# The last token tiles of a transformer trunk: tile 2's LayerNorm on VectorE with plain stores, in place of ScalarE with an adding transfer

## The chip, the cores and the metric

One core of one Trainium2 chip runs the whole program. The metric is the device time of one execution in microseconds. The kernel before takes 1698.73 us (median of three runs, 1698.60 to 1699.02).

A core has five engines that run their own instruction queues and wait for each other by semaphores: TensorE (PE in the profile; PEld is its weight load), VectorE (DVE), ScalarE (ACT), GpSimd (POOL) and SyncE (SP). SyncE here does nothing but issue transfers. Transfers issued by SyncE run in the hardware queue (q1), those issued by GpSimd in the software queue (q0). Only the ones from GpSimd can add to what already lies at the destination. Both queues share the same 16 transfer engines.

## The reference, cut to what matters

The reference is a trunk of two layers on 512 tokens of width 1024. Each layer ends with a channel sublayer and a LayerNorm over it:

```python
def layer_norm(x, g, b):
    mu = jnp.mean(xf, axis=-1, keepdims=True)
    var = jnp.mean(jnp.square(xf - mu), axis=-1, keepdims=True)
    y = (xf - mu) * lax.rsqrt(var + LN_EPS) * g + b

for i in range(DEPTH):
    ...                                       # token sublayer: attention, retention, merge, LayerNorm 1
    ffn = conv_glu_ffn(x, w_up[i], conv_w[i], conv_b[i], w_down[i])
    ple = jax.nn.sigmoid(x @ w_ple_gate[i]) * (p[i] @ w_ple_proj[i])
    x = layer_norm(DEEPNORM_ALPHA * x + ffn + ple, ln2_g[i], ln2_b[i])
return x
```

The change concerns the very last line of the last layer: `layer_norm(...)` with `ln2_g` and `ln2_b`, whose result is the program's output.

## The kernel before, in words

All matrix products are float32. Each operand is split into two parts, `hi` (a cast on ScalarE) and `lo` (a subtraction on VectorE), and each product is three matmuls. Weights come in pieces of 512 KB: SyncE loads them in the order of one long list (`Stream`), and GpSimd adds a second piece to some of them with adding transfers (`Stream.add`), since the down projection and two other products use a block scheme with seven products (`a`, `c`, `t1`, `t2`, `d`, `t3`, `t4`) in place of eight.

Tokens are rows. The 512 tokens are four tiles of 128 partitions. For the last sublayer of a layer, `R[0]` to `R[3]` hold the four row tiles (128 x 1024) of the sum that goes into LayerNorm 2. The down projection runs in three segments (`SEGS`), and in the last one (`fin`) of the last layer (`last`) each `R[t]` becomes final and is normalised. Within these parts every engine's instructions stand in the order in which the code issues them (`_Ordered`), so the order of the calls is the order of the work on each engine.

The halves of the tiles become final in this order: tiles 0 and 1 after product `d`, tiles 2 and 3 after `t4`, which yields tile 2 first and tile 3 half a product later. The functions that the end is made of:

- `stats(t, cb)`: VectorE's sums of one half of tile t. `moments(t)`: mean and variance from the two halves, then `rstd_of`: variance + eps on VectorE (`ve`), its power -1/2 on GpSimd (`rstd`).
- `norm_gb(t)`, for tiles 0 and 1: ScalarE computes (R - mean) * rstd in one pass, GpSimd multiplies by the gain `g2c`.
- `send(t)`: GpSimd issues an adding transfer of `R[t]` (512 KB) to `out`. For this, rows of `out` are filled with the bias beforehand: at line 1129, at the start of the last layer's channel sublayer, SyncE writes the bias row to all rows of tiles 0, 1 and 2.
- `norm_g(t)`: VectorE, whole tile: (R - mean) * gain. `norm_b(t)`: VectorE, in two halves: R * rstd + bias, each half followed by a plain transfer (256 KB) that SyncE issues.

In the kernel before, tiles 0 and 1 take `norm_gb` and `send`. Tile 2 takes `norm_g` on VectorE, a scaling by rstd on ScalarE, and `send(2)`. Tile 3 takes `norm_g` and `norm_b`. On GpSimd the end of the queue is: rstd of tile 2, `send(1)`, `send(2)`, rstd of tile 3.

SyncE's transfers rotate through eight completion semaphores, and each one waits, where needed, for the transfer that used its semaphore last. At the end of the program (line 1584) every engine drains, SyncE waits for all transfers to have landed, and two barriers follow.

Of the kernel before, what the change touches and what calls it, by code (L numbers as in the profile page):

```python
# [10 lines left out]
AF = mybir.ActivationFunctionType  # L11
# [91 lines left out]
def trunk(tc, wpack, x_nat, x_tr, head, p_tr, rpb, decay, ln_par, ln_col, conv, cos_t, sin_t, dist, xi_d, zd, mask, ident_d, out):  # L103
    nc = _Engines(tc)
# [3 lines left out]
    with ExitStack() as es:  # L108
# [14 lines left out]
        def nm(s):  # L123
            cnt[0] += 1
            return f"{s}_{cnt[0]}"
# [4 lines left out]
        def unit_f(s, shape=(P, 1024)):  # L130
            return up.tile(list(shape), F32, tag="u", name=nm(s))
# [273 lines left out]
        def drain(g):  # L405
            for _ in g:
                pass
# [171 lines left out]
        def ple_half(l, cb):  # L579

            if cb == 0:
                pk[:] = [unit_f("pp") for _ in range(4)]

            def keep(t, ps):
                nc.scalar.copy(pk[t][:, cb * 512:(cb + 1) * 512], ps)

            lh = lambda k, s, t: ptr[l][k][:, s, t * P:(t + 1) * P]
            if l or cb:
                drain(gemm_n(lh, 1, [], post=keep))
                return  # L590

            hi, lo = ws.get()
            pss = [bank("gn") for _ in range(4)]
            for k in range(2):
                r = slice(k * 512, (k + 1) * 512)
                for t in range(4):
                    for s in range(2):
                        nc.tensor.matmul(pss[t], lh(k, s, t), hi[:, r], start=k == s == 0, stop=False)
                for t in range(4):
                    nc.tensor.matmul(pss[t], lh(k, 0, t), lo[:, r], start=False, stop=k == 1)  # L600
                    if k:
                        keep(t, pss[t])
# [11 lines left out]
        for l in range(DEPTH):  # L614
# [511 lines left out]

            if last:

                for t in range(3):
                    nc.sync.dma_start(out[t * P:(t + 1) * P, :], ln_par[l, 3:4, :].to_broadcast([P, D]))  # L1130

            R = [unit_f("R") for _ in range(4)]
# [155 lines left out]
            for s, n in enumerate(SEGS):  # L1288
# [39 lines left out]
                def into(t, c, ps, op=ALU.add):  # L1328
                    nc.vector.tensor_tensor(R[t][:, c], R[t][:, c], ps, op)

                def stats(t, cb):
                    if fin:
                        nc.vector.bn_stats(st[t][:, cb, :], R[t][:, (N1, N2)[cb]])
# [8 lines left out]
                mv, rs, nmr = {}, {}, {}  # L1342

                def moments(t):
                    mv[t] = small("mv", 2)
                    nc.vector.bn_aggr(mv[t], st[t])
                    rs[t] = rstd_of(mv[t][:, 1:2], LN_EPS, 1)

                def norm(t, R=R):
                    nc.vector.tensor_scalar(R[t], R[t], mv[t][:, 0:1], rs[t], op0=ALU.subtract, op1=ALU.mult)  # L1350
# [10 lines left out]
                def send(t, R=R):  # L1361

                    nc.gpsimd.dma_start(out[t * P:(t + 1) * P, :], R[t], accum_op=ALU.add)

                def norm_g(t, R=R):
                    nc.vector.scalar_tensor_tensor(R[t], R[t], mv[t][:, 0:1], g2c, op0=ALU.subtract, op1=ALU.mult)

                def norm_b(t, R=R):
                    for c in (N1, N2):
                        nc.vector.scalar_tensor_tensor(R[t][:, c], R[t][:, c], rs[t], b2c[:, c], op0=ALU.mult, op1=ALU.add)  # L1370
                        nc.sync.dma_start(out[t * P:(t + 1) * P, c], R[t][:, c])

                def out_pair(t, xt, xf, R=R):
                    h = t // 2
                    for k in range(4):
                        if k % 2 == 0:
                            xf[h, k // 2] = unit_f("xf", (P, 2, 2, 256))
                        ps = bank("tr")
                        f = xf[h, k // 2][:, k % 2]
                        for q in range(2):  # L1380
                            for i in range(2):
                                nc.tensor.transpose(ps[:, (2 * q + i) * P:(2 * q + i + 1) * P], R[t + i][:, (k + 4 * q) * P:(k + 4 * q + 1) * P], ident)
                        for q in range(2):
                            kk = k + 4 * q
                            nc.scalar.activation(f[:, q, :], ps[:, q * 256:(q + 1) * 256], AF.Identity, bias=gb[:, 1, kk:kk + 1], scale=gb[:, 0, kk:kk + 1])
                    yield
                    for k in range(4):
                        ts = slice(t * P, (t + 2) * P)
                        split(xt[:, k:k + 5:4, 0, ts], xt[:, k:k + 5:4, 1, ts], xf[h, k // 2][:, k % 2])
                    yield  # L1390
# [46 lines left out]
                for k in BOUND if not last else ("t4a", "t4b"):  # L1437
                    if k[0] == "p":
                        ple_half(l + 1, int(k[1]))
                    elif k == "tr":  # L1440
                        ws.xw = None
                        xt = xp.tile([P, 8, 2, 512], F32R, tag="xt", name=nm("xt"))
                        xf = {}
                        drain(out_pair(0, xt, xf))
                    else:
                        i = "ab".index(k[2]) + 2
                        next(t4)
                        into(i, N1, x4[i - 2])
                        stats(i, 0)
                        moments(i)  # L1450
                        if not last:
                            norm(i)
                            nc.sync.dma_start(scr[i * P:(i + 1) * P, :], R[i])
                        elif i == 2:
                            send(1)
                            norm_g(2)
                            nc.scalar.activation(R[2], R[2], AF.Copy, scale=rs[2])
                            send(2)
                if last:
                    norm_g(3)  # L1460
                    norm_b(3)
            pending = out_pair
# [125 lines left out]
```

## Time and profile before

| | us |
|---|---|
| runs, median (lowest to highest of 3) | 1698.73 (1698.60 to 1699.02) |
| the profiled execution's own time | 1698.33 |
| its span, first to last instruction | 1696.5 |
| TensorE busy | 1679.7 |
| end of the last matmul, from the span's start | 1681.7 |
| end of VectorE's last instruction | 1687.7 |
| `send(0)`, `send(1)`, `send(2)`: issued by GpSimd at | 1678.42, 1682.06, 1684.73 |
| and landed after | 5.3, 6.6, 6.7 |
| plain halves of tile 3: issued by SyncE at | 1687.03, 1687.69 |
| and landed after | 4.9, 4.9 |
| pre-fill of tiles 0, 1, 2 with the bias: issued from 1271.91, landed after | 12.2, 14.6, 14.8 |

Times within the profile are counted from the span's start. The profiled execution is one run; its time is 1.8 us above its span, and 0.4 us below the median of the three runs. In rows of the timeline the columns are start, duration, engine, line, operation, output <- inputs, shape, count, and in brackets the idle time before it and what ended it. Most operations carry line 86, the helper that fixes the order, so they are told apart by their tiles: `R` is a row tile, `lng` and `lnb` gain and bias, `mv` the moments. A `q` behind an engine's name (POOLq, SPq) is its instruction queue: issuing, waiting and draining, not computing.

### The profile page before, as it was taken

How to read it: one execution, taken by the hardware profiler on the slowest of the kernel's cores; microseconds unless marked ns; L12 is line 12 of the kernel's file. 1: busy time of each engine (PE TensorE's matmuls, PEld its weight loads, DVE VectorE, ACT ScalarE, POOL GpSimd, SP SyncE). 2: the span in 40 equal slices, each digit the busy share in tenths (PEclk: the TensorE clock that was granted, in tenths of full speed). 3: DMA queues.
4: the chain of work that ended last, by engine and by line, in shares of the span. 5: the costliest groups of instructions: out<-in, count | busy, mean ns of one | idle time of the engine just before them, and what ended most of it. 6: DMA issues, size and time to landing. Idle time of an engine off the chain costs nothing.

```text
span 1696.5 us, 20952 instructions
## 1 busy us (share of the span) xinstructions
PE 1679.7 (99%) x7895; PEld 1404.1 (83%) x7895; DVE 1251.7 (74%) x1870; ACT 903.5 (53%) x1345; POOL 125.7 (7%) x143
## 2 busy tenths in 40 slices
PE   9999999999999999999999999999999999999996
PEld 7888888888888888888888888888888888888885
DVE  6768778657787767667875787776678887676777
ACT  6755557654366444345575654666444573443442
POOL 1100000000200100000112000000002010010012
PEclk9999999999999999999999999999999999999998
DMA  8953222344656535526779322232466464274274
GB/s 299 257 161 106 87 81 90 103 143 152 196 137 160 123 113 161 140 98 181 205 210 231 117 78 91 72 109 93 161 212 194 123 174 115 84 200 123 82 214 90
DMA packets 73397, 244.52 MB, mean 144 GB/s; under 512 B 8528, under 2 KB 11088, under 8 KB 73296
## 3 DMA queue, kind: packets, MB, share of 16 engines
q1 hardware_dynamic: 58464, 191.27, 32.9%
q0 software_dynamic: 14832, 51.91, 17.4%
q8 instruction: 62, 1.02, 0.2%
q14 instruction: 39, 0.32, 0.1%
HBM read 228.47 MB, written 14.16 MB: 143 GB/s over the span
## 4 chain that ended last, share of the span: by engine, by line
PE 92%; DVE 3%; issue 2%; DMA 1%; ACT 1%; POOL 1%; SPq 0%; POOLq 0%; DVEq 0%; ACTq 0%
PE gt L86 29%; PE u L86 12%; PE gt L363 8%; PE gt L364 8%; PE gt L365 8%; PE v L86 6%; PE w L86 3%; PE gn L365 3%; PE gn L363 3%; PE gn L364 3%; PE x L86 1%; PE gn L86 1%; PE na L983 1%; PE pt L971 1%; DVE lo L86 1%
## 5 line engine op out<-in xcount | busy, mean ns | idle before, releaser
L86 PE MATMUL gt<-x1t,hi 128*128 128x512 f32 x1408 | 433.4, 389 | 0.0
L86 PEld LDWEIGHTS gt<-x1t,hi 128*128 128x128 f32 x1408 | 264.3, 188 | 54.9
L86 PE MATMUL gt<-x1t,lo 128*128 128x512 f32 x704 | 274.1, 389 | 0.1
L86 DVE TENSOR_TENSOR lo<-raw,hi 128x1024 fp32r<-128x1024 f32 (+1 forms) x155 | 185.5, 1207 | 44.7 <-ACT hi L86 44.2
L86 DVE SCALAR_TENSOR_TENSOR ca<-gt,cw,ca 128x511 f32<-128x511 f32 x176 | 131.8, 749 | 79.0 <-ACT ca L86 75.9
L156 ACT CAST hi<-raw 128x1024 fp32r<-128x1024 f32 x96 | 100.9, 1051 | 146.9 <-issue 80.5
L86 ACT CAST hi<-raw 128x1024 fp32r<-128x1024 f32 (+1 forms) x155 | 159.7, 1040 | 34.3 <-PE u L86 14.4
L363 PE MATMUL gt<-xt,hi 128*128 128x512 f32 x416 | 163.5, 393 | 0.0
L157 DVE TENSOR_TENSOR lo<-raw,hi 128x1024 fp32r<-128x1024 f32 x96 | 117.4, 1223 | 62.3 <-ACT hi L156 61.7
L364 PE MATMUL gt<-xt,hi 128*128 128x512 f32 x416 | 162.2, 390 | 0.0
L365 PE MATMUL gt<-xt,lo 128*128 128x512 f32 x416 | 162.1, 390 | 0.0
L86 PEld LDWEIGHTS gt<-x1t,lo 128*128 128x128 f32 x704 | 132.1, 188 | 28.3 <-DVE lo L86 1.0
L86 ACT ACTIVATE ca<-gt,cw 128x512 f32<-128x512 f32 x88 | 68.6, 780 | 131.0 <-PE gt L86 131.0
L86 DVE TENSOR_TENSOR lo<-rawa,hi 128x1024 fp32r<-128x1024 f32 x90 | 104.7, 1175 | 42.8 <-ACT hi L86 42.3
L86 ACT CAST hi<-rawa 128x1024 fp32r<-128x1024 f32 x90 | 90.0, 1015 | 37.9 <-DMA rawa<-in_wpack 18.8
L365 PEld LDWEIGHTS gt<-xt,lo 128*128 128x128 f32 x416 | 78.1, 188 | 16.6
L363 PEld LDWEIGHTS gt<-xt,hi 128*128 128x128 f32 x416 | 78.2, 188 | 15.0
L364 PEld LDWEIGHTS gt<-xt,hi 128*128 128x128 f32 x416 | 78.2, 188 | 14.8
L86 POOL DMA_DIRECT2D rawa<-in_wpack x68 | 61.3, 916 | 340.0 <-DVE lo L86 295.2
L86 PE MATMUL gt<-xt,hi 128*128 128x512 f32 x192 | 59.2, 389 | 0.0
L86 PE MATMUL v<-hi,sa 128*128 128x512 f32 x176 | 56.1, 389 | 0.0
L413 POOL TENSOR_TENSOR rstd<-ve,mhalf 128x2 f32<-128x2 f32 (+1 forms) x24 | 23.3, 972 | 369.0 <-DVE ve L411 369.0
(322 smaller groups left out, 3556.2 us busy)
## 6 DMA issues: line engine op xcount, KB each, us to landing
raw<-in_wpack SPq DMA_DIRECT2D x247, 512.0 KB, 3.8
rawa<-in_wpack POOLq DMA_DIRECT2D x66, 512.0 KB, 6.4
rawa<-in_wpack SPq DMA_DIRECT2D x22, 512.0 KB, 6.4
rawt<-in_wpack SPq DMA_DIRECT2D x22, 512.0 KB, 6.5
rawt<-in_wpack POOLq DMA_DIRECT2D x22, 512.0 KB, 7.7
r_scr<-pp SPq DMA_DIRECT2D x8, 512.0 KB, 9.8
g_scr<-sga SPq DMA_DIRECT2D x16, 256.0 KB, 4.4
sab<-g_scr SPq DMA_DIRECT2D x16, 256.0 KB, 4.0
```

Source lines behind the costliest of these rows:

```text
L86: r = f(*a, **k)
L156: nc.scalar.copy(hi, src)
L157: nc.vector.tensor_sub(lo, src, _f(hi))
L363: nc.tensor.matmul(ps, lh, rh, start=start, stop=False, skip_group_check=more)
L364: nc.tensor.matmul(ps, lh, rl, start=False, stop=False, skip_group_check=more)
L365: nc.tensor.matmul(ps, ll, rh, start=False, stop=stop, skip_group_check=more)
L413: nc.gpsimd.tensor_tensor(r, v, mhalf[:, :n], ALU.pow)
L971: nc.tensor.transpose(ps[:, i * P:(i + 1) * P], S[:, g * 256 + bb * P:g * 256 + (bb + 1) * P], ident)
L983: nc.tensor.matmul(ov[kt], lv, pt[kt // 2][:, sp_, c], start=i == 0 and sp_ == 0, stop=i == 3 and sp_ == 1)
```

## The change

Tile 2 is treated as tile 3 is. Its rows of `out` are not filled with the bias beforehand, ScalarE's scaling and `send(2)` are gone, and `norm_b(2)` is called where tile 3's moments have been computed and `norm_g(3)` is about to be. Tiles 0 and 1 stay as they are.

```diff
             if last:
-                for t in range(3):
+                for t in range(2):
                     nc.sync.dma_start(out[t * P:(t + 1) * P, :], ln_par[l, 3:4, :].to_broadcast([P, D]))
...
                         elif i == 2:
                             send(1)
                             norm_g(2)
-                            nc.scalar.activation(R[2], R[2], AF.Copy, scale=rs[2])
-                            send(2)
                 if last:
+                    norm_b(2)
                     norm_g(3)
                     norm_b(3)
```

On the engines this gives: SyncE one transfer less at the start of the sublayer and two more at the end, ahead of tile 3's two; ScalarE one instruction less; GpSimd one transfer less, so that rstd of tile 3 follows `send(1)`; VectorE two half-tile instructions more, between tile 3's `ve` and `norm_g(3)`. The order of everything else is the same.

## The prediction

> **What bounds the kernel now.** I read the page first, then the last 18 us of the chain of waits, the order of work there, the landings of the transfers to `out`, and the instructions that close the program (line 1584).
>
> The page: TensorE is busy 99% of the span.
>
> ```profile
> span 1696.5 us, 20952 instructions
> ...
> PE 1679.7 (99%) x7895; PEld 1404.1 (83%) x7895; DVE 1251.7 (74%) x1870; ACT 903.5 (53%) x1345; POOL 125.7 (7%) x143
> ```
>
> So only two things can move the time: a hole in TensorE's row, or the tail behind its last matmul, which ends at 1681.7. The tail is 14.8 us. The chain of waits there (start, duration, what) runs through GpSimd: its rstd of tile 2, ScalarE's scaling of tile 2, the issue of the third adding transfer, and only then VectorE's last step.
>
> ```profile
> 1681.41 1.85 POOL rstd L86
> 1683.26 0.02 issue
> 1683.28 1.16 ACT R L86
> 1684.44 0.29 issue
> 1684.73 0.86 POOL out L86
> 1685.59 0.64 POOLq L1584
> 1686.23 0.03 issue
> 1686.25 0.75 DVE R L86
> ```
>
> The timeline shows the same end by engine: the reader is to see VectorE idle for 0.45 us at 1685.8, because rstd of tile 3 stands in GpSimd's queue behind the transfer at 1684.73.
>
> ```profile
> 1684.53 1.28 DVE L86 SCALAR_TENSOR_TENSOR R<-R,mv,lng 128x1024 f32<-128x1024 f32 x1
> 1684.73 0.86 POOL L86 DMA_DIRECT2D out<-R  x1 [0.61 <-ACT R L86]
> 1685.30 0.92 POOL L86 TENSOR_TENSOR rstd<-ve,mhalf 128x1 f32<-128x1 f32 x1
> 1686.25 1.41 DVE L86 SCALAR_TENSOR_TENSOR R<-R,rstd,lnb 128x512 f32<-128x512 f32 x2 [0.45 <-POOL rstd L86]
> 1687.03 1.11 SPq L86 DMA_DIRECT2D out<-R  x2
> ```
>
> But compute is over at 1687.7 and the span lasts to 1696.5. The closing instructions of line 1584 (count, then ns min/median/max, then first and last start):
>
> ```profile
> L1584 POOLq DRAIN  x3: 40/93/10982, 1684.7 to 1696.2; - x3
> L1584 SPq DRAIN  x3: 7/7/7, 1692.8 to 1696.0; - x3
> ```
>
> SyncE, which waits for every transfer, is done at 1692.9. GpSimd's first drain starts at 1684.7 and takes 10.98, so it ends at 1695.7; 0.77 of barriers follow. What SyncE waited for (total, times, longest) agrees: 3.3 us for transfers, then 3.0 at the barrier.
>
> ```profile
> SPq L1584 <- DMA out<-R: 4.1, 3, 3.3
> SPq L1584 <- PEq L1584: 3.5, 2, 3.0
> ```
>
> So **GpSimd's drain ends the program**, 2.8 us behind everything else. It ends 4.25 us after the third adding transfer has landed (issued 1684.73, landing 6.74 later: 1691.47) and 9.5 us after GpSimd's last instruction (rstd of tile 3, 1686.22). VectorE's drain, in contrast, ends 0.05 us after its last instruction.
>
> The plain transfers: the two halves of tile 3 landed 4.9 us after issue.
>
> ```profile
> L86 SPq DMA_DIRECT2D out<-R x2: 344/397/450, 1687.0 to 1687.7; - x2
> ...
> DMA to landing us min/median/max: 4.9/4.9/5.0
> ```
>
> The same 256 KB from SBUF to HBM, with nothing beside it, landed in 2.0.
>
> ```profile
> L781 SPq DMA_DIRECT2D g_scr<-sga x1: 326/326/326, 1032.5 to 1032.5; - x1
> ...
> DMA to landing us min/median/max: 2.0/2.0/2.0
> ```
>
> From 1688.4 to 1690.5 the adding queue (q0) had the engines, and only 6 plain packets ran (queue, packets, MB, share of the engines).
>
> ```profile
> q0 software_dynamic: 109, 0.42, 101.0%
> q1 hardware_dynamic: 6, 0.01, 1.8%
> ```
>
> **The change part by part.** Its order of instructions is otherwise unchanged on all five engines.
>
> *The pre-fill of tile 2's rows (one of three at 1271.9).* SyncE issues 0.8 us less and 512 KB less moves. What hides it: TensorE was busy 40.00 of 40 us from 1260 to 1300 and 99.93 of 100 in the next 100, so no gain. Every later SyncE transfer shifts by one in the rotation of eight completion semaphores, but each still waits for the transfer eight before it. If the cover went, the holes of that stretch are the measure: 0.07 us. I take 0, with ±0.3 from the spread of the runs (1698.60 to 1699.02).
>
> *ScalarE's scaling (1.15) and the third adding transfer (0.86 of GpSimd, 512 KB).* Both leave the chain. On the transfer engines the adding queue's work from 1688.4 to 1690.9 disappears.
>
> *rstd of tile 3.* GpSimd's queue is free at 1684.1, when the second adding transfer is issued (1682.06 + 2.05); the input is ready at 1684.61. The four rows of this operation in the tail take 0.55, 0.56, 0.92 and 1.83, so it ends between 1685.2 and 1686.5 instead of 1686.22. VectorE needs it at 1687.2 (next step), so either end is hidden from VectorE. The Trainium skill ("GPSIMD Engine Reference", Key points) says that GpSimd contends for its SBUF interfaces with VectorE instructions that have two SBUF inputs, as the added ones do; the trace agrees (2.07 against 1.28 for the two `norm_g`), and by it rstd would be at the 1.83 end.
>
> *Two half-tile steps on VectorE (`norm_b(2)`).* They stand directly behind the `ve` of tile 3 and ahead of `norm_g(3)`. rstd of tile 2 has been there since 1683.3, so they start at 1684.53 where `norm_g(3)` started. Their pitch is 0.67 (1686.25 to 1686.92), so `norm_g(3)` runs 1685.87 to 1687.15 and the halves of `norm_b(3)` start at 1687.18 and 1687.85. That is +1.34 for the two steps, less the 0.45 idle, with 0.03 of waiting: **+0.93**. The last half is ready at 1688.59.
>
> *Four plain transfers in place of two.* SyncE issues at 1685.3, 1686.0, 1687.96 and 1688.62 (0.03 behind each half, as before); an issue is 0.34 to 0.45, so none queues on SyncE. The second adding transfer holds the engines from 1684.5 to 1688.4 and still lands at 1688.66: its packets were ahead of the third one's. Behind it four halves at 0.64 each (the spacing of the two landings before, 1691.98 and 1692.62) are through at 1691.0; by the lone 2.0 us the last would land at 1690.6; by the 4.93 of before, at 1693.55. I take 1691.0, as the backlog that made the 4.93 is gone. SyncE's list then ends 0.26 later (1692.62 to 1692.88 before): 1691.3, ends 1690.9 and 1693.8.
>
> *GpSimd's drain.* No row shows it without the third transfer. Tied to the last adding transfer, it ends 4.25 behind 1688.66, at 1692.9. Tied to GpSimd's last instruction, it ends 9.5 behind 1685.2 to 1686.5, at 1694.7 to 1696.0. Without anything to wait for it could be as short as the other drains of the row (0.04 to 0.09), and then SyncE's 1691.3 decides. I take the first: the program's first drain on GpSimd, ahead of any adding transfer, took 0.19, and the two behind the long one 0.09 and 0.04, so the length comes from something outstanding, and the transfers are what GpSimd had outstanding.
>
> A rule that speaks against this choice: the Trainium skill ("Perfetto Trace Analysis", DMA Instruction, SWDGE) has a GpSimd transfer end for GpSimd when its descriptors are written, not when data lands. The 0.86 us rows agree with that for the instruction; for the drain, no run here shows which. By that rule the drain would not see the landing, and the sum would be the second value, -1.0 instead of -2.8.
>
> **The sum.** Drain end 1695.72 to 1692.9: -2.8. SyncE's end (1691.3) is hidden behind it. Barriers as before, 0.77. The span becomes 1693.7, and with the 1.8 around it (1698.33 - 1696.5) the profiled execution 1695.5. The median of the runs, 1698.73, is 0.4 above the profiled one: 1698.73 - 2.8 = **1695.9**. Its own range: -1.9 if SyncE's end is 1693.8; -4.1 if the second adding transfer lands 5.3 after its issue, as the first did, and not 6.6: 1694.6 to 1696.9.
>
> A measurement of this kernel can tell about 0.2% from no change, that is 3.4 us; below 1695.3 counts as faster, above 1702.1 as slower.
>
> **The rivals.**
>
> *The drain lets go (faster).* It is no longer than SyncE's list: the end is 1691.0 to 1691.3 + 0.77, a span of about 1692.1, -4.4: 1694.3. For it: the other drains are short. Against it: the drain outlasted the landing by 4.25 before, and there is still an adding transfer that lands only 2.6 us before SyncE is done. It decides if the drain's lag falls under 2.6.
>
> *The drain counts from GpSimd's last instruction (same).* rstd of tile 3 ends 1.0 earlier: -1.0, 1697.7; with rstd at its slow end, +0.3 and 1699.0. For it: one execution can't tell the lag of 9.5 from that of 4.25, and VectorE's drain does follow its last instruction. Against it: the short drains. The rule of the Trainium skill above ("Perfetto Trace Analysis") leads here too.
>
> *The plain halves become the last thing (other side).* If the drain waits until the transfer engines are quiet for 3.1 us (1692.62 to 1695.72) and the halves keep their 4.93, the 0.93 of VectorE goes straight to the end: 1688.62 + 4.93 + 3.1 + 0.77 = 1697.4 of span, +0.9: 1699.7. It decides once the halves' landing is above 4.0. Against it: at 1688.6 the adding queue is empty.
>
> *A hole upstream (slower).* The shifted semaphores hold one weight load until TensorE runs dry; to be over 0.2% it must cost 3.4 + 2.8 us, against 0.07 us of holes in 1300 to 1681 now.
>
> **How the numbers follow.** Forecast 0.54, of which 0.06 is beyond -3.4; drain lets go 0.24; GpSimd's last instruction 0.14; plain halves last 0.05; hole upstream 0.03. Faster: 0.24 + 0.06 = 0.30. Slower: 0.03, with 0.01 for what I have not thought of: 0.04. Within: 0.66. The range from 1694.0 (0.3 under the fastest case) to 1697.9 leaves out the slow half of the third case, the fourth and the fifth, and some 0.03 at the low end: under 0.2.
>
> **What would show it.** Right: VectorE's last step 0.9 later, without the 0.45 idle; the halves of tile 3 landing in 2.0 to 2.5 us; GpSimd's drain ending near 1692.9 and SyncE's barrier wait falling from 3.0 to about 1.6. Wrong: a drain that ends 9.5 behind rstd, or one shorter than SyncE's list; the second adding transfer landing later than 1688.7 because plain packets now share the engines, which would move the drain with it one for one; or any idle TensorE between 1271 and 1681.

## The result, and the profile after

The changed kernel takes 1695.76 us (median of 18 runs, 1695.20 to 1696.34), the one before 1699.09 in the runs beside it (18 runs, 1698.22 to 1700.29). The ratio is 0.9981, with a 95% interval of 0.9973 to 0.9988: 3.3 us less, just inside the 0.2% that was set as the bound of no change; the interval leaves 1 out, so the gain is there, though small. The forecast was 1695.9.

The profiled execution has a span of 1694.1 us where the one before had 1696.5. Its last matmul ends 0.34 later (1682.05 against 1681.70), so the times of the tail are best read from there: the tail was 14.78 us and is 12.04, that is 2.74 less.

The page of the changed kernel, its first two lines of numbers: TensorE's work is the same.

```profile
span 1694.1 us, 20954 instructions
...
PE 1680.1 (99%) x7895; PEld 1404.4 (83%) x7895; DVE 1252.7 (74%) x1872; ACT 900.5 (53%) x1344; POOL 124.9 (7%) x142
```

The last part of its chain of waits (start, duration, what). GpSimd and ScalarE are gone from it; it is VectorE alone:

```profile
1685.08 2.62 DVE R L86 x3
1687.70 0.03 issue
1687.73 0.02 DVEq L86
1687.75 0.04 issue
1687.80 0.75 DVE R L86
```

The timeline of the same stretch. The idle time that VectorE had ahead of its last step is gone, `norm_b(2)` stands ahead of `norm_g(3)`, and SyncE issues four halves:

```profile
1682.59 2.05 POOL L86 DMA_DIRECT2D out<-R  x1
...
1685.08 1.42 DVE L86 SCALAR_TENSOR_TENSOR R<-R,rstd,lnb 128x512 f32<-128x512 f32 x2
1685.24 1.01 POOL L86 TENSOR_TENSOR rstd<-ve,mhalf 128x1 f32<-128x1 f32 x1 [0.59 <-DVE ve L86]
1685.86 3.71 SPq L86 DMA_DIRECT2D out<-R  x4
1686.41 1.28 DVE L86 SCALAR_TENSOR_TENSOR R<-R,mv,lng 128x1024 f32<-128x1024 f32 x1
1687.80 1.41 DVE L86 SCALAR_TENSOR_TENSOR R<-R,rstd,lnb 128x512 f32<-128x512 f32 x2
```

The instructions that close the program (line 1583 now; count, ns min/median/max, first and last start), and what SyncE waited for:

```profile
L1583 POOLq DRAIN  x3: 40/102/8110, 1685.2 to 1693.8; - x3
L1583 SPq DRAIN  x3: 7/7/7, 1691.9 to 1693.6; - x3
```

```profile
SPq L1583 <- PEq L1583: 2.1, 2, 1.6
SPq L1583 <- DMA out<-R: 1.7, 3, 0.6
```

GpSimd's first drain still ends the program, at 1685.19 + 8.11 = 1693.30, but 1.4 us behind SyncE's list (1691.92) and no longer 2.8. SyncE's wait at the barrier is down from 3.0 to 1.6, as forecast.

The landings of the transfers to `out`: the second adding one, issued at 1682.59,

```profile
DMA to landing us min/median/max: 6.5/6.5/6.5
```

and the two plain halves of tile 3, issued at 1688.58 and 1689.24:

```profile
DMA to landing us min/median/max: 2.4/2.5/2.5
```

So the last adding transfer lands at 1689.09, and the drain ends 4.21 behind that; before it was 4.25 behind the third. The halves of tile 3 land in 2.5 instead of 4.9: from 1688.7 to 1691.6 one packet of the adding queue ran beside 528 plain ones. Ahead of that, from 1685 to 1688.3, the second adding transfer had the engines, though two plain halves had been issued by 1686.9 (queue, packets, MB, share of the engines):

```profile
q0 software_dynamic: 126, 0.50, 99.1%
q1 hardware_dynamic: 2, 0.00, 0.4%
```

### The profile page after: what moved, and what is told of

Its sections match the earlier page's. It is cut to its first block, busy times and chain, and to the rows that moved or that the text cites. A ratio compares the mean times of both kernels' runs of the same rounds, so it can differ in the third digit from the quotient of the medians.

```text
span 1694.1 us, 20954 instructions
## 1 busy us (share of the span) xinstructions
PE 1680.1 (99%) x7895; PEld 1404.4 (83%) x7895; DVE 1252.7 (74%) x1872; ACT 900.5 (53%) x1344; POOL 124.9 (7%) x142
## 4 chain that ended last, share of the span: by engine, by line
PE 97%; DVE 2%; ACT 1%; issue 0%; DVEq 0%; ACTq 0%
PE gt L86 32%; PE u L86 13%; PE gt L363 8%; PE gt L364 8%; PE gt L365 8%; PE v L86 7%; PE w L86 3%; PE gn L365 3%; PE gn L364 3%; PE gn L363 3%; PE x L86 2%; PE gn L86 1%; PE na L983 1%; PE pt L971 1%; PE o L365 1%; PE o L364 1%
```

## The experiments

The theory on record: what ends the program is GpSimd's drain, and that ends a fixed 4.2 us behind the landing of the last transfer GpSimd issued. Its main rival: the drain counts from GpSimd's last instruction. The times of all tails stand in one table; the ends of drains are start plus duration, and landings are issue plus time to landing, from the traces. SyncE's list is done when it has waited for every transfer, ahead of the closing barriers.

| run | GpSimd's last instruction ends | its last transfer lands | drain ends | behind the instruction | behind the landing | SyncE's list done | span | tail behind the last matmul |
|---|---|---|---|---|---|---|---|---|
| before | 1686.22 | 1691.47 | 1695.72 | 9.50 | **4.25** | 1692.88 | 1696.5 | 14.78 |
| changed | 1686.24 | 1689.09 | 1693.30 | 7.06 | **4.21** | 1691.92 | 1694.1 | 12.04 |
| e1 | 1686.23 | 1688.92 | 1693.13 | 6.90 | **4.21** | 1691.61 | 1693.9 | 11.65 |
| e2 | 1685.50 | 1667.55 | 1691.59 | **6.10** | 24.04 | 1691.12 | 1692.4 | 10.07 |
| e3 | 1690.52 | 1688.68 | 1696.77 | **6.26** | 8.09 | 1691.43 | 1697.6 | 15.41 |
| e4 | 1686.50 | 1693.18 | 1697.43 | 10.93 | **4.25** | 1694.67 | 1698.2 | 16.52 |
| e5 | 1686.13 | 1688.19 | 1692.40 | **6.27** | **4.21** | 1690.93 | 1693.2 | 11.53 |
| e6 | 1686.77 | 1691.56 | 1695.81 | 9.04 | **4.25** | 1693.13 | 1696.6 | 14.37 |
| e7 | 1686.33 | 1687.79 | 1692.58 | **6.26** | 4.79 | 1691.58 | 1693.4 | 11.02 |
| e8 | 1686.25 | 1688.95 | 1693.16 | 6.91 | **4.21** | 1691.76 | 1693.9 | 11.67 |
| e9 | 1683.50 | 1687.69 | 1691.90 | 8.40 | **4.21** | 1691.67 | 1692.7 | 10.39 |
| e10 | 1685.33 | 1687.10 | 1691.58 | **6.26** | 4.48 | 1690.56 | 1692.4 | 11.00 |

In bold is the one of the two that the drain's end fits. In every run the span ends 0.76 to 0.78 behind the drain.

**e1: the pre-fill back**

```diff
-                for t in range(2):
+                for t in range(3):
                     nc.sync.dma_start(out[t * P:(t + 1) * P, :], ln_par[l, 3:4, :].to_broadcast([P, D]))
```

> The changed kernel, but with the bias written ahead to tile 2's rows too, as in the kernel before (the plain halves overwrite it at the end). My theory (the tail alone moved, and GpSimd's drain follows the landing of the last adding transfer by 4.2 us): nothing changes, span 1694.1 within 0.5, TensorE idle nowhere between 1260 and 1681. Rival (part of the gain came from 512 KB less on the transfer engines at 1272): the matmuls end later by that part, up to 2.4 us, and the span goes back towards 1696.5.

Measured: 1695.43 us, ratio to the kernel before 0.9981 (0.9972 to 0.9990), span 1693.9. The ratio is that of the changed kernel, so the removed pre-fill is worth nothing that these runs can show. Busy time by stretch in this run (the stretch, its length, then TensorE's busy time) shows it covered, here for 1260 to 1300:

```profile
1260.00:1300.00 40.00, 40.00 (x190) 33.30 (x190) 27.86 (x41) 11.45 (x22) 8.23 (x8) 1.00 0.82 245
```

**e2: no adding transfer at the end**

```diff
                 def send(t, R=R):
-                    nc.gpsimd.dma_start(out[t * P:(t + 1) * P, :], R[t], accum_op=ALU.add)
+                    nc.sync.dma_start(out[t * P:(t + 1) * P, :], R[t])
```

> The changed kernel, with the stores of tiles 0 and 1 issued by SyncE as plain transfers at the places of the adding ones; their bias is left out of the output, all other work stays. The last adding transfer is then one of weights, which landed near 1667. My theory: GpSimd's drain ends with its last instruction, rstd of tile 3, near 1686.5; SyncE's list sets the end: last half issued near 1689.2, landed 2.0 to 2.5 later, list done near 1691.9, span 1692.3 to 1692.8, that is 1.3 to 1.8 below the changed kernel. Rival (the drain counts a fixed time from GpSimd's last instruction, 7.1 in the changed kernel and 9.5 in the one before): drain ends between 1693.3 and 1696, span 1694 to 1696.7.

Measured: 1693.64 us, ratio 0.9971 (0.9960 to 0.9982), span 1692.4. The span came out as the theory had it, but not for its reason. The drain did not end with rstd of tile 3 at 1685.5:

```profile
L1583 POOLq DRAIN  x3: 40/93/7067, 1684.5 to 1692.1; - x3
L1583 SPq DRAIN  x3: 7/7/7, 1691.1 to 1691.8; - x3
```

It ends at 1691.6, 6.1 behind GpSimd's last instruction and 0.5 behind SyncE's list, although everything that GpSimd had issued had landed 24 us earlier. The rival's constant count from the last instruction (7.1 or 9.5) is not it either. So there is a second bound, which the theory lacked: the drain takes some 6 us behind the last instruction with nothing to wait for. The time agrees with the theory's only because that bound happens to lie near the end of SyncE's list.

**e3: GpSimd's last instruction later, no transfer moved**

```diff
                 if last:
                     norm_b(2)
                     norm_g(3)
+                    for _ in range(6):
+                        nc.gpsimd.tensor_tensor(small("late", 1), rs[2], mhalf[:, :1], ALU.pow)
                     norm_b(3)
```

> The changed kernel with six more one-column powers on GpSimd behind rstd of tile 3, whose results nobody reads: GpSimd's last instruction ends about 3 us later (near 1689.5), no transfer moves. My theory: the drain still ends 4.2 behind the landing of the second adding transfer, near 1693.3, and the span stays at 1694.1 within 0.5. Rival (the drain counts from GpSimd's last instruction): drain and span end 3 us later, near 1697.

Measured: 1699.24 us, ratio 1.0003 (0.9993 to 1.0013), span 1697.6. The theory falls here: it had the span unchanged, and it rose by 3.5. (The six powers took 4.42 and not 3.) In this run's timeline and closing instructions, six one-column powers that nobody waits for move the end of the program:

```profile
1685.11 1.01 POOL L86 TENSOR_TENSOR rstd<-ve,mhalf 128x1 f32<-128x1 f32 x1 [0.59 <-DVE ve L86]
1686.09 4.42 POOL L86 TENSOR_TENSOR late<-rstd,mhalf 128x1 f32<-128x1 f32 x6
```

```profile
L1585 POOLq DRAIN  x3: 40/102/10615, 1686.2 to 1697.3; - x3
```

The drain ends 6.26 behind the last of them. But the rival on record falls as well, for it had a constant lag, and the lag was 9.50 before and 7.06 in the changed kernel.

**e4: a third adding transfer again, and nothing else of the old way**

```diff
                     norm_g(3)
+                    nc.gpsimd.dma_start(scr[0:P, :], g2c, accum_op=ALU.add)
                     norm_b(3)
```

> The changed kernel with one adding transfer of 512 KB more, issued by GpSimd behind rstd of tile 3, from the gain tile to a scratch tensor in HBM that nobody reads any more: the third adding transfer comes back without ScalarE's scaling and with the two steps on VectorE kept. It is issued near 1686.3, runs behind the second one and should land at 1691.4 to 1692. My theory: the drain ends 4.2 behind that, at 1695.6 to 1696.2, and the span is 1696.4 to 1697.0, 2.3 to 2.9 above the changed kernel, while the plain halves land later than before but are no bound. Rival (the drain counts from GpSimd's last instruction, or the gain came from the shorter chain through ScalarE): span within 1 us of 1694.1.

Measured: 1700.11 us, ratio 1.0010 (1.0000 to 1.0019), span 1698.2. The whole gain is gone and more, without ScalarE in the chain and without another user of the data. The transfer landed 7.6 after its issue, over 1 us later than expected:

```profile
L86 POOL DMA_DIRECT2D x_scr<-lng x1: 882/882/882, 1685.6 to 1685.6; - x1
...
DMA to landing us min/median/max: 7.6/7.6/7.6
```

The drain followed it by 4.25, at 1697.4, 10.9 behind GpSimd's last instruction:

```profile
L1584 POOLq DRAIN  x3: 40/93/12598, 1684.8 to 1697.9; - x3
```

**e5: the third transfer plain, the engines' work as before**

```diff
                             nc.scalar.activation(R[2], R[2], AF.Copy, scale=rs[2])
-                            send(2)
+                            nc.sync.dma_start(out[2 * P:3 * P, :], R[2])
```

(This one starts from the kernel before.)

> The kernel before with one line changed: tile 2, normalised and scaled on VectorE and ScalarE as before, is stored by a plain transfer that SyncE issues in place of the third adding one (its rows then lack the bias). This takes the transfer away and leaves the work on the engines. My theory: the drain ends 4.2 behind the landing of the second adding transfer, near 1693, and the span is 1693.7 to 1694.3, the same as the changed kernel within 0.5 although VectorE ends about 0.9 earlier: the 0.93 us on VectorE is hidden. Rival (VectorE's 0.93 is part of the changed kernel's end): the span is 0.9 below the changed kernel's.

Measured: 1695.69 us, ratio 0.9983 (0.9974 to 0.9991); the changed kernel beside it (e8) 1695.54. The profiled span of 1693.2 is 0.9 below the changed kernel's 1694.1, which is the rival's number; but in this profile the last matmul ended early, at 1681.65 (1682.05 in the changed kernel, 1682.26 in e8). The tails behind it are 11.53 here and 11.67 in e8, and the 11 runs of each kernel have the same median span, 1693.8. So the transfer alone carries the change, and VectorE's later end (1687.58 here, 1689.21 in e8) is hidden to within 0.15. In this run the two bounds of the drain, its tie to the last landing and the one that e2 showed, fall on the same time: 1688.19 + 4.21 and 1686.13 + 6.27 are both 1692.40.

```profile
L1584 POOLq DRAIN  x3: 40/93/7831, 1684.6 to 1692.9; - x3
```

**e6: the late transfer plain**

```diff
                     norm_g(3)
+                    nc.gpsimd.dma_start(scr[0:P, :], g2c)
                     norm_b(3)
```

> The run with the late transfer once more, but plain: GpSimd issues 512 KB from the gain tile to scratch behind rstd of tile 3, without adding. It should land near 1690 (half of the adding one's time on the engines, behind the second adding one at 1688.6). Theory as it stands (the drain waits for whatever GpSimd issued): drain near 1694.2, span near 1695. Rival (only adding transfers are waited for): drain 1693.3, span 1694.1.

Measured: 1698.19 us, ratio 0.9997 (0.9988 to 1.0006), span 1696.6. The transfer landed later than expected, at 1691.56, and the drain ended 4.25 behind it. So the drain waits for a plain transfer too, if GpSimd issued it; the plain halves that SyncE issued landed later still here (the last at 1692.92), and the drain does not count from them.

**e7: the second send ahead of rstd of tile 2**

```diff
                         into(i, N1, x4[i - 2])
                         stats(i, 0)
+                        if last and i == 2:
+                            send(1)
                         moments(i)
...
                         elif i == 2:
-                            send(1)
                             norm_g(2)
```

> The changed kernel with the second adding transfer called ahead of the moments of tile 2, so that on GpSimd it stands ahead of rstd of tile 2. Nothing is left out. It should be issued near 1682.4 in 0.9 instead of 2.05 us and land 5.3 after that, near 1687.7 instead of 1689.1; rstd of tile 2 is then ready near 1684, VectorE wants it at 1685.1. My theory: the drain ends near 1692.0, as SyncE's list does, and the span is 1692.8, 1.3 below the changed kernel and 3.7 below the one before. Rival (rstd of tile 2 comes too late for VectorE): VectorE's last step and the last half's landing are later by the wait, and the span gains less than 0.5.

Measured: 1694.60 us, ratio 0.9976 (0.9967 to 0.9985), against 1695.54 of the changed kernel beside it (e8). The issue of the second adding transfer takes 0.89 and not 2.05, and it lands at 1687.79. The rival does not show: rstd of tile 2 ended at 1684.15, VectorE took it up at 1685.17, and VectorE's end is 6.94 behind the last matmul, as in e1. But the span is 1693.4 and not 1692.8: behind the landing the drain would have ended at 1692.0, and it ends at 1692.58, 6.26 behind rstd of tile 3. The second bound has taken over.

```profile
L1584 POOLq DRAIN  x3: 40/102/7308, 1685.3 to 1693.1; - x3
```

**e8: the changed kernel beside the others**

> The changed kernel itself, beside the others on the same chip, to compare with: span 1694.1 and time 1695.8 within 0.6; ratio to the kernel before 0.998.

Measured: 1695.54 us, ratio 0.9982 (0.9973 to 0.9990), span 1693.9.

These eight gave a new theory: the drain ends at the later of two times, 4.2 behind the last landing of what GpSimd issued, and 6.3 behind GpSimd's last instruction. e9 put it to a test that it could fail: with both made early, the landing has to decide again.

**e9: rstd of tiles 2 and 3 off GpSimd** (on top of e7)

```diff
+                    if last and t >= 2:
+                        ve, sd[t] = small("ve", 1), small("sd", 1)
+                        nc.vector.tensor_scalar_add(ve, mv[t][:, 1:2], LN_EPS)
+                        nc.scalar.activation(sd[t], ve, AF.Sqrt)
+                        return
                     rs[t] = rstd_of(mv[t][:, 1:2], LN_EPS, 1)
...
                 def norm_b(t, R=R):
+                    rs[t] = small("rstd", 1)
+                    nc.vector.reciprocal(rs[t], sd[t])
```

> The run with the early second send, and rstd of tiles 2 and 3 taken off GpSimd: ScalarE's square root and VectorE's reciprocal in its place, nothing left out. New theory from the runs so far: GpSimd's drain ends at the later of two times, 4.2 behind the last landing of what GpSimd issued, and 6.3 behind GpSimd's last instruction. Here the last instruction is the second send, over near 1683.6, so the second time is near 1689.9; the second send lands near 1687.8, so the first is 1692.0; SyncE's list is done near 1691.9, as the two reciprocals (0.15 each) stand on VectorE's way. The drain ends at 1692.0, the span is 1692.8, 0.6 below the run with the early send alone (1693.4). Rival (the drain has a shortest length of about 7 from some other start, and the square root's table load delays VectorE): span 1693.4 or more.

Measured: 1694.42 us, ratio 0.9975 (0.9965 to 0.9985), span 1692.7, tail 10.39. The drain starts at 1682.59 and ends at 1691.90, 4.21 behind the landing; the first bound is back, to 0.1 us of the expected 1692.0. SyncE's list is now done only 0.2 earlier:

```profile
L1591 POOLq DRAIN  x3: 40/102/9312, 1682.6 to 1692.4; - x3
L1591 SPq DRAIN  x3: 7/7/7, 1691.6 to 1692.2; - x3
```

The square root's table load (1.28) ran on an idle ScalarE at 1677.35, so it delayed nobody.

**e10: the early send once more**

> The run with the early second send once more, beside the one without late GpSimd work: span 1693.4, drain ended by GpSimd's last instruction (rstd of tile 3) plus 6.3; ratio to the kernel before 0.9976.

Measured: 1694.73 us, ratio 0.9977 (0.9968 to 0.9986); drain 6.26 behind rstd of tile 3, as expected; span 1692.4, 1.0 below the 1693.4 expected, as the last matmul ended 1.0 earlier than in e7; tail 11.00. The tails of e9 and e10 differ by 0.6, the medians by 0.3; at this spread the runs alone would not part e9 from e10. Both are below the changed kernel: of the versions that compute the full output, e9 has the lowest median, 4.2 us under the kernel before.

## Why the prediction was right, point by point

**What bounds the kernel.** Right. The tail alone moved: holes of TensorE from 1260 to 1681 are below 0.1 in the changed kernel and in e1, and the drain ended the program in all twelve profiles.

**The pre-fill at nothing.** Right (e1).

**VectorE's +0.93.** Its last instruction ended 5.96 behind the last matmul before and 7.16 now: 1.20. In this profile the size was off by 0.3, the most of it (0.18) a `norm_g(2)` that took 2.25 in place of 2.07. In e1 and e8 the end is 6.94 and 6.95 behind the last matmul, 0.98 later than before, so the forecast size was right to 0.05. The cover held: SyncE's list, which follows VectorE, ended 1.4 ahead of the drain.

**rstd of tile 3.** Forecast to end between 1685.2 and 1686.5, measured 1686.24. It took 1.01 beside `norm_b(2)`, not the 1.83 that the contention weighed in the prediction would have given it. For VectorE the runs bear that contention out: in e2 GpSimd's multiply is over before `norm_g(2)` starts, and `norm_g(2)` takes 1.28 and not 2.03 to 2.25.

**The plain halves.** Last landing forecast at 1691.0 and the list at 1691.3; measured 1691.71 and 1691.92, of which 0.34 is the later last matmul and about 0.3 VectorE. The choice between 2.0 and 4.93 of landing was near the lower end, at 2.5. The rival in which the halves become the last thing did not come up: it had the drain 3.1 behind the last half, and it ended 1.6 behind (0.4 in e9).

**The second adding transfer.** Forecast to land at 1688.66 as before, measured at 1689.09, or 0.09 later if counted from the last matmul. That is past the 1688.7 that the prediction named as a sign of being wrong, but not for its reason: only two plain packets ran from 1685 to 1688.3, and in e1 and e8 the landing is 0.3 earlier than before, counted the same way.

**The drain.** The forecast took the first of three values, tied to the last landing, and for this kernel that is what happened: forecast 1692.9, measured 1693.30, 0.06 off with the later matmul taken out. The reason given for the choice was half right. The drain waits for landings: e4, e6 and e9 show it. But the step "without anything to wait for it could be as short as the other drains" failed: e2 had nothing to wait for and its drain took 6.1. The first rival (the drain lets go, 1694.3) could therefore not happen with rstd of tile 3 where it stands. The second rival had a true part, a count from GpSimd's last instruction, with 6.3 in place of 9.5; in the changed kernel that bound is at 1692.5, only 0.8 under the one that decided. The forecast hit with that little to spare.

The rule of the Trainium skill that was weighed ("Perfetto Trace Analysis", DMA Instruction, SWDGE) puts the profile's end of a GpSimd transfer where its last descriptor is written, not where the data has moved. The rows agree: in the changed kernel the issue ends at 1684.65, rstd of tile 3 behind it at 1686.24, and the landing comes at 1689.09. The step from there to a drain that does not see the landing does not hold: the drain at the end of the program does wait for it.

**The time.** The drain's terms give 2.74 in the profiles, against 2.8 forecast; the medians of the runs lie 3.3 apart (interval 2.0 to 4.6 by the ratio). Three profiles of the changed tail (changed, e1, e8) give 12.04, 11.65 and 11.67, so up to 3.1 is the tail; the kernel before has one profile here, and whether its 14.78 varies as much stays open. The spans of the runs beside each other (33 before, 11 in e8) have medians of 1696.8 and 1693.8, so 3.0 apart. The forecast of the time itself was only 0.14 off, and that is partly luck: it started from 1698.73, the kernel before took 1699.09 in the runs beside the change, and the gain came out 0.5 larger.

## What to carry to other kernels

Look at what the last drain of each engine waits for, not only at the last compute and the last landing: here the engine with 7% of the span in work ended the program in every version. Near the end of a program like this one let GpSimd issue nothing that lands late and execute nothing late, even if nobody reads its result; SyncE's list, in contrast, was done at most 0.6 behind its last landing in all twelve profiles. When one such bound goes, work out at once where the next one stands: the 1.3 us forecast for the early send came out as 0.6 in the tail because the second bound was 0.6 behind the first.

## What the runs showed of the hardware that was not expected

- GpSimd's closing drain, in this kernel, ends at the later of 4.21 to 4.25 us behind the last landing of its own transfers (adding or plain) and 6.10 to 6.27 us behind its last instruction, in twelve of twelve profiles; the rule was drawn from the first ten and held in e9 and e10. What it does in those 4 and 6 us is not shown. Wherever the second time decided, the last instruction was a one-column power; whether another one, or the issue of a transfer, does the same is not shown. The drain at the start of the program, before any transfer, took 0.18 to 0.19, and the two that follow the long one 0.04 to 0.10.
- The same 512 KB adding transfer took GpSimd 2.05 us to issue when it stood behind rstd of tile 2, and 0.89 when it stood ahead of it (e7, e9), with VectorE's `norm_g(2)` running beside it both times. The records overlap: in the changed kernel 1.18 of the 2.05 lie ahead of the end of rstd of tile 2 (1683.78). Behind rstd's end 0.87 are left, as long as the whole issue in e7.
- Plain halves issued while an adding transfer held the engines landed after 3.8 us (tile 2, changed kernel) and 4.9 (tile 3, before); with the adding ones landed or gone it was 2.0 (e2) to 2.5 (tile 3, changed kernel).
